# Down projections by seven products per 2x2 block, with low weight parts added in transit and one PSUM pool

## The chip, the core and the metric

One core of a Trainium2 chip runs the whole program in one launch. The engines are PE (the matrix engine, with its weight loads shown as PEld), DVE, ACT and POOL (element-wise work) and SP (which issues DMAs); ACT and POOL can issue DMAs too. The metric is the device time of one execution in microseconds, lower is better.

## What is computed

512 tokens with 1024 features pass two model blocks of two layers each. In the reference, cut to what matters here:

```python
def sqrelu_mlp(h, w1, w2):                 # first block, both layers; 1024 -> 4096 -> 1024
    return jnp.square(jax.nn.relu(h @ w1)) @ w2
def swiglu(h, w_gate, w_up, w_down):       # second block, both layers; 1024 -> 2816 -> 1024
    return (jax.nn.silu(h @ w_gate) * (h @ w_up)) @ w_down
# first block, layer l:  x += conformer_conv or fox_attention
#                        x += memory_cross_attention
#                        x += sqrelu_mlp(rmsnorm(x, norm_ff_g[l]), ff_w1[l], ff_w2[l])
# second block, layer i: x += short_conv_mixer or dilated_attention_mixer
#                        x += swiglu(rms_norm(x, ffn_norm[i]), gate, up, down)
```

All of it is in 32-bit floats.

## The kernel before

Activations lie transposed: features on 128 partitions, 512 tokens along a row, so that `x` is eight tiles `x[0..7]` of 128x512. Every matrix product keeps 32-bit precision by three matmuls in the reduced format FP32R: operands are split into a high part (a rounded copy) and a low part (the value less its high part), and `mm3` (L173) issues high x high, high x low and low x high into one PSUM bank.

`load_weights` (L146) has SP load 1 MB of weights (eight row tiles, 256 columns) into `raw`, a ring of three buffers. `split_weights` (L163) makes the parts of each 128 columns: ACT copies the high part `whi` (L169), DVE subtracts the low part `wlo` (L170). `gemm_steps` (L182) takes two output tiles at a time: for each it issues 8 x 3 matmuls of 128x128 weights by 128x512 activations, then calls `evac`.

In `ff_sqrelu` (L694) the 4096 hidden features are taken in four chunks of eight tiles. For each chunk a first product (w1) fills `hid`: DVE scales and clips out of PSUM (L706), ACT squares (L708), and `split_act` makes `ahi` (ACT) and `alo` (DVE, L224). A second product (w2) then multiplies the chunk by 1024x1024 weights, and `residual` (L591) adds each of the eight results to `x` on DVE (L593). In `swiglu` (L718) the chunks have 8, 8 and 6 tiles, and gate and up products stand for w1. The w2 product of one chunk is called a down projection stage below: 8 x 8 x 3 = 192 matmuls of 512 columns.

PSUM has eight banks of 128x512. `banks(g, s, t)` (L111) is called where an attention or a convolution begins; it closes the pool of PSUM tiles and opens another with the new division. The first tile of a new pool waits until those of the pool before have been read.

The order of matmuls is that of the program (L91 to L95). That of the other engines is set by the framework's scheduler, from the dependences and its own cost estimates; each engine works off its list in order, an instruction that waits holds up those behind it. In `fox` (L1107) POOL issues the loads of `fr` and `fb` and multiplies `fr` by a gain (L1119); before, in its list, stand eight gain multiplies on attention weights (L782, in `parts_of`). `fw` (L1123) is made of `fr` by ACT and DVE and is the operand of the first matmuls there. The end of the first block is `last1` (L1283), which adds the last result (L1284) and scales it.

Of the kernel before, what the change touches and what calls it, by code (L numbers as in the profile page):

```python
# [9 lines left out]
F32 = mybir.dt.float32  # L10
# [72 lines left out]
def model_kernel(tc, a, c_mats, c_onehot, c_lnn, out):  # L83
# [24 lines left out]

    psum = {}

    def banks(g, s, t):  # L111

        if psum:
            psum["stack"].close()
        psum["stack"] = ExitStack()
        psum["pool"] = pool("ps", stack=psum["stack"], space=bass.MemoryType.PSUM)
        psum["bufs"] = {"g": g, "s": s, "t": t}

    def bank(tag="g"):
        return psum["pool"].tile([P, 512], F32, name="ps_" + tag, tag=tag, bufs=psum["bufs"][tag])  # L120

# [41 lines left out]
    def split_weights(view, shape):  # L163
# [18 lines left out]
    def gemm_steps(specs, acts, evac, first=False, norm=None):  # L182

        nk = len(acts)
        for c in range(0, len(specs), 2):
            w = prepare(specs[c : c + 2], nk)
            nm = len(w)  # L190
# [400 lines left out]
    def residual(st):  # L591
# [102 lines left out]
    def ff_sqrelu(l, st, last=None):  # L694
        nrm = Norm(st)
        with ExitStack() as s:
            ap = pool("fact", 22, s)
            fp = pool("fftmp", stack=s)
            h = [gained_act(hp_all, x[k], gain("norm_ff_g", l)[:, k : k + 1]) for k in range(KT)]
            st2 = Stats()  # L700
            for hc in range(FF1 // D):
                hid = []

                def evac(m, acc, hid=hid):
                    t = fp.tile([P, T], F32, name="t", tag="t", bufs=4)
                    nc.vector.scalar_tensor_tensor(t, acc, 0.0, nrm.b, op0=OP.max, op1=OP.mult)  # L706
                    u = fp.tile([P, T], F32, name="u", tag="u", bufs=4)
                    nc.scalar.activation(u, t, AF.Square)  # L708
                    hid.append(split_act(ap, u))

                gemm(cols(a["ff_w1"][l], 0, hc * D), h, evac, first=hc == 0, norm=nrm, hooks=nrm.hooks() if hc == 0 else ())
                final = hc == FF1 // D - 1
                gemm(
                    cols(a["ff_w2"][l], hc * D, 0), hid, (last or residual(st2)) if final else residual(None), first=True
                )
        return st2

    def swiglu(l, st, last=None, finish=None):  # L718
        nrm = Norm(st)
        banks(4, 2, 2)  # L720
        with ExitStack() as s:
            ap = pool("gact", 22, s)
# [3 lines left out]
            wg, wu, wd = a["ffn_w_gate_2"][l], a["ffn_w_up_2"][l], a["ffn_w_down_2"][l]  # L726
            m0 = 0
            for n in (8, 8, 6):
                hid = []
                for j in range(n):  # L730
                    c = (m0 + j) * P
                    res = {}

                    def evac(m, acc, res=res, hid=hid):
                        if m == 0:
                            t = fp.tile([P, T], F32, name="t", tag="t", bufs=4)
                            nc.vector.tensor_tensor(t, acc, nrm.b, op=OP.mult)  # L737
                            g = fp.tile([P, T], F32, name="g", tag="g", bufs=4)
                            nc.scalar.activation(g, t, AF.Silu)  # L739
                            nc.gpsimd.tensor_tensor(g, g, nrm.b, op=OP.mult)  # L740
                            res[0] = g
# [12 lines left out]
                m0 += n
        return st2

    def heads_attention(specs, fold, h, nrm, bias_of, hp, wo, prologue, ahead=0):
# [19 lines left out]
        def parts_of(owner, view, nk, width, f, cuts, pl, tag):  # L777
# [92 lines left out]
        def v_steps(grp):  # L870
# [9 lines left out]
            def products():  # L880
                flush(("v", grp))
                for tt in range(2):
                    b = bank("g")
                    for t2 in range(2):
                        t = tt * 2 + t2
                        for k in range(KT):
# [491 lines left out]
    def finish(specs, acts):  # L1378
# [78 lines left out]
```

## Time and profile before

| | |
|---|---|
| median of 3 runs | 2654.21 us (2652.49 to 2655.27) |
| profiled execution | 2655.16 us, its span 2653.4 us |
| PE busy | 2600.3 us (98%), 12521 matmuls |
| DVE, ACT, POOL busy | 1489.7 (56%), 1097.9 (41%), 548.8 us (21%) |
| share of PE in the chain that ended last | 82% |

The span is the time from the first to the last recorded instruction. The trace gives each instruction a start and a duration; matmuls are pipelined, so that their records overlap, and the distance from one start to the next tells what one costs. "Idle before" a group is the time in which its engine stood still just ahead of it, with the event that ended it. A granted clock of 1.00 is 2.4 GHz, 0.50 is 1.2 GHz. A DMA's landing is counted from its issue to its completion.

### The profile page before, as it was taken

The numbers are of one execution on the slowest core, as the hardware profiler recorded it, in microseconds if no ns is written. First come the engines' busy times: TensorE is split into PE (matmuls) and PEld (weight loads), VectorE is DVE, ScalarE is ACT, GpSimd is POOL, SyncE is SP. The second block draws the span as 40 slices with busy tenths as digits, with TensorE's granted clock in tenths as the row PEclk, the third lists the DMA queues.
The fourth block names the chain that finished last, engine by engine and source line by source line (L and its number), as shares of the span: only waits on it lengthen the run. The fifth ranks groups of instructions, "written<-read, shape, count | busy, mean of one in ns | idle before, by whom it ended". The sixth has DMA issues, their size and how long they took to land.

```text
span 2653.4 us, 32283 instructions
## 1 busy us (share of the span) xinstructions
PE 2600.3 (98%) x12521; PEld 2178.7 (82%) x12521; DVE 1489.7 (56%) x2215; ACT 1097.9 (41%) x1843; POOL 548.8 (21%) x585
## 2 busy tenths in 40 slices
PE   8999999999999999999999999999999999999999
PEld 6889888888878787888888788888888888788888
DVE  6995564433557887554344665433335777643333
ACT  6755443322437675342223322322224666422223
POOL 5862110000226532110000511211112221211111
PEclk9999999999999999999999999999999999999999
DMA  7255133333322222233333393333324232233331
GB/s 211 78 194 181 56 96 96 98 103 101 95 74 72 80 96 72 72 111 96 95 97 96 87 166 109 90 100 101 96 83 119 85 88 88 77 96 98 96 87 56
DMA packets 319320, 264.82 MB, mean 100 GB/s; under 512 B 6980, under 2 KB 304512, under 8 KB 319168
## 3 DMA queue, kind: packets, MB, share of 16 engines
q1 hardware_dynamic: 316112, 258.15, 33.4%
q10 hardware_dynamic: 2480, 4.33, 0.5%
q8 instruction: 99, 1.62, 0.3%
q0 software_dynamic: 576, 0.28, 0.1%
q14 instruction: 53, 0.43, 0.1%
HBM read 251.16 MB, written 11.57 MB: 99 GB/s over the span
## 4 chain that ended last, share of the span: by engine, by line
PE 82%; DVE 6%; POOL 4%; issue 4%; ACT 2%; DMA 1%; SPq 0%; ACTq 0%; POOLq 0%; DVEq 0%
PE ps_g L92 76%; PE ps_s L92 3%; POOL pa L433 2%; PE ps_t L92 2%; PE ps_t L95 1%; DVE wlo L170 1%; DVE ps_s L425 1%; DVE alo L236 1%; DVE x L593 1%; POOL sall L994 1%; POOL raw L782 0%; DVE x L938 0%; DMA raw<-in_conv_pw_w 0%; DVE wlo L795 0%; DVE x L1286 0%
## 5 line engine op out<-in xcount | busy, mean ns | idle before, releaser
L92 PE MATMUL ps_g<-ahi,whi 128*128 128x512 f32 x3052 | 1195.2, 392 | 10.8 <-DVE x L593 5.8
L92 PE MATMUL ps_g<-alo,whi 128*128 128x512 f32 x3052 | 1188.0, 389 | 1.6 <-DVE alo L236 1.6
L92 PE MATMUL ps_g<-ahi,wlo 128*128 128x512 f32 x3052 | 1188.0, 389 | 0.0
L169 ACT CAST whi<-raw 128x1024 fp32r<-128x1024 f32 (+2 forms) x384 | 384.1, 1007 | 1163.1 <-PE ps_g L92 1103.3
L92 PEld LDWEIGHTS ps_g<-ahi,whi 128*128 128x128 f32 x3052 | 574.7, 188 | 129.6 <-issue 11.1
L92 PEld LDWEIGHTS ps_g<-ahi,wlo 128*128 128x128 f32 x3052 | 574.2, 188 | 120.3 <-DVE wlo L795 0.2
L92 PEld LDWEIGHTS ps_g<-alo,whi 128*128 128x128 f32 x3052 | 574.8, 188 | 117.5 <-DVE alo L236 2.4
L170 DVE TENSOR_TENSOR wlo<-raw,whi 128x1024 fp32r<-128x1024 f32 (+2 forms) x384 | 462.7, 1210 | 75.5 <-ACT whi L169 70.8
L593 DVE TENSOR_TENSOR x<-ps_g,x 128x512 f32<-128x512 f32 x144 | 99.1, 689 | 337.5 <-PE ps_g L92 337.5
L260 POOL TENSOR_TENSOR ssq<-ssq,sq 128x512 f32<-128x512 f32 x78 | 119.4, 1531 | 609.2 <-issue 311.9
L740 POOL TENSOR_TENSOR g<-g,rb 128x512 f32<-128x512 f32 x44 | 74.2, 1687 | 555.2 <-ACT g L739 555.2
L706 DVE SCALAR_TENSOR_TENSOR t<-ps_g,rb 128x512 f32<-128x512 f32 x64 | 44.0, 691 | 161.0 <-PE ps_g L92 160.3
L782 POOL TENSOR_TENSOR raw<-raw,gcols 128x512 f32<-128x512 f32 x48 | 53.8, 1145 | 302.1 <-DMA raw<-in_kvf_w 302.1
L433 POOL TENSOR_TENSOR pa<-pa,pr 128x512 f32<-128x512 f32 x80 | 111.8, 1400 | 18.7 <-ACT pa L429 8.2
L744 DVE TENSOR_TENSOR u<-ps_g,g 128x512 f32<-128x512 f32 x44 | 30.4, 691 | 145.3 <-PE ps_g L92 141.1
L425 DVE SCALAR_TENSOR_TENSOR ps_s<-u,gcols,ps_s 128x512 f32<-128x512 f32 x152 | 104.2, 744 | 0.2
L994 POOL TENSOR_SCALAR sall<-sall,rs 128x512 f32<-128x512 f32 (+3 forms) x128 | 75.9, 605 | 128.5 <-DVE rs L993 117.4
L795 DVE TENSOR_TENSOR wlo<-raw,whi 128x512 fp32r<-128x512 f32 x128 | 94.4, 765 | 13.2 <-ACT whi L792 13.2
L792 ACT CAST whi<-raw 128x512 fp32r<-128x512 f32 x128 | 74.1, 620 | 53.3 <-PE ps_g L92 47.1
L737 DVE TENSOR_TENSOR t<-ps_g,rb 128x512 f32<-128x512 f32 x44 | 30.4, 691 | 112.8 <-PE ps_g L92 112.8
L236 DVE SCALAR_TENSOR_TENSOR alo<-x,gcols,ahi 128x512 fp32r<-128x512 f32 x64 | 82.3, 1299 | 13.8 <-ACT ahi L235 13.8
L224 DVE TENSOR_TENSOR alo<-u,ahi 128x512 fp32r<-128x512 f32 x116 | 81.7, 707 | 2.7 <-ACT ahi L223 2.7
(244 smaller groups left out, 2838.0 us busy)
## 6 DMA issues: line engine op xcount, KB each, us to landing
raw<-in_ff_w SPq DMA_DIRECT2D x64, 1024.0 KB, 5.0
raw<-in_ffn_w_gate SPq DMA_DIRECT2D x44, 512.0 KB, 4.0
raw<-in_ffn_w_up SPq DMA_DIRECT2D x44, 512.0 KB, 5.3
raw<-in_ffn_w_down SPq DMA_DIRECT2D x16, 1024.0 KB, 5.0
raw<-in_conv_pw_w SPq DMA_DIRECT2D x16, 512.0 KB, 5.4
raw<-in_mem_wk SPq DMA_DIRECT2D x8, 1024.0 KB, 5.1
raw<-in_mem_wv SPq DMA_DIRECT2D x8, 1024.0 KB, 5.9
raw<-in_mem_wq SPq DMA_DIRECT2D x8, 1024.0 KB, 4.9
```

The lines of the kernel that those rows point to most:

```text
L92: tc.keep_in_program_order(nc.tensor.matmul(*args, **kw))
L169: nc.scalar.copy(hi, view)
L170: nc.vector.tensor_tensor(lo, view, hi.bitcast(F32), op=OP.subtract)
L224: nc.vector.tensor_tensor(lo, src, hi.bitcast(F32), op=OP.subtract)
L236: nc.vector.scalar_tensor_tensor(lo, src, g, hi.bitcast(F32), op0=OP.mult, op1=OP.subtract)
L260: nc.gpsimd.tensor_tensor(self.ssq, self.ssq, dst, op=OP.add)
L425: nc.vector.scalar_tensor_tensor(acc, u[:, j : j + T], tapw(j), acc, op0=OP.mult, op1=OP.add)
L433: nc.gpsimd.tensor_tensor(pa, pa, pr, op=OP.add)
L593: nc.vector.tensor_tensor(x[m], acc, x[m], op=OP.add)
L740: nc.gpsimd.tensor_tensor(g, g, nrm.b, op=OP.mult)
L795: nc.vector.tensor_tensor(w[1][:, k0 : k0 + n, :], v, w[0][:, k0 : k0 + n, :].bitcast(F32), op=OP.subtract)
L994: pinned(nc.gpsimd.tensor_scalar(s, s, rs[:, i : i + 1], 1.0, op0=OP.mult, op1=OP.mult))
```

## The change

The down projections of all but the last chunk of each MLP (three in each `ff_sqrelu`, two in each `swiglu`, ten stages in all) are computed by a scheme of seven products. A hidden pair (two tiles of hidden features, index k) and an output pair (two output tiles, index j, four of them) form a 2x2 block of weights a11, a12, a21, a22; the tokens are taken in two halves of 256. Each block needs seven products, of sums of weights by sums of activations, instead of eight: 4 x 7 x 4 x 3 matmuls of 256 columns per stage.

`Hidden` makes the activations' sums (DVE) and their parts; the seven entries of `bhi` and `blo` are the four quarters less one and four combinations. `Seven.weights` prepares one output pair. Two groups of weights enter as they are: b (a11) and a (a12 and a22). For these `split_by_transfer` has ACT write the high part, ACT write its negative into `wlo`, and POOL issue a DMA that adds the weights, read once more from DRAM, onto it. The other groups, c and d, are sums, made in place in `raw` (POOL one, DVE three) and split as before. Results go to `x` or to accumulators `acc`, and `combine` adds these to `x` during the first product of the last chunk.

All eight PSUM banks are now tiles of one pool that stays open; `banks` only deals them out anew, the least recently used first. In the fox stage the gain multiplies of one key/query pair and that of `fr` go from POOL to DVE.

The diff, cut to its core:

```diff
+    ps_pool = pool("ps", stack=psum, space=bass.MemoryType.PSUM)
+    by_use = list(range(8))
     def banks(g, s, t):
-        if psum:
-            psum["stack"].close()
...
+        free = list(by_use)
+        for tag, n in (("g", g), ("s", s), ("t", t)):
+            rings[tag], free = free[:n], free[n:]
     def bank(tag="g"):
...
+        return ps_pool.tile([P, 512], F32, name="ps_" + tag, tag=f"bank{i}", bufs=1)
+    def split_by_transfer(view, src, shape):
+        slot = "ab"[turn[0] // 2 % 2]
+        turn[0] += 1
+        hi = wsp.tile(shape, F32R, name="whi", tag="whi" + slot, bufs=2)
+        lo = wsp.tile(shape, F32R, name="wlo", tag="wlo" + slot, bufs=2)
+        nc.scalar.copy(hi, view)
+        nc.scalar.activation(lo, hi.bitcast(F32), AF.Identity, scale=-1.0)
+        nc.gpsimd.dma_start(lo, src, accum_op=OP.add)
+        return hi, lo
...
+    SEVEN = (
+        ("b", None, 0, "A", 1),
+        ("a", 0, 2, "B", 1),
+        ("a", 1, 6, "D", 1),
+        ("c", 1, 4, "C", 1),
+        ("c", 0, 3, "C", 0),
+        ("d", 1, 5, "A", 0),
+        ("d", 0, 1, "B", 0),
+    )
+    class Hidden:
...
+        def quarters(self):
+            f = self.raw
+            d = self.ap.tile([P, 4, HALF], F32, name="bdif", tag="bdif", bufs=1)
+            nc.scalar.copy(self.hi[:, 0:3, :], f[:, 1:4, :])
+            nc.vector.tensor_tensor(
+                d[:, 0:2, :], f[:, 1:3, :], f[:, 0:1, :].to_broadcast([P, 2, HALF]), op=OP.subtract
+            )
+            nc.vector.tensor_tensor(d[:, 2, :], f[:, 2, :], d[:, 0, :], op=OP.add)
+            nc.vector.tensor_tensor(d[:, 3, :], d[:, 2, :], f[:, 3, :], op=OP.subtract)
+            nc.scalar.copy(self.hi[:, 3:7, :], d)
+            for part, src in ((slice(0, 3), f[:, 1:4, :]), (slice(3, 7), d)):
+                nc.vector.tensor_tensor(
+                    self.lo[:, part, :], src, self.hi[:, part, :].bitcast(F32), op=OP.subtract
+                )
+    class Seven:
...
+        def weights(self, src, r0, j, h):
+            raw = load_weights([(src, r0, 2 * j * P), (src, r0, (2 * j + 1) * P)], 2 * h)
...
+            w = {
+                "b": split_by_transfer(a11, rows[:, :, 0, 0:P], [P, h, P]),
+                "a": split_by_transfer(odd, rows[:, :, 1, :], [P, h, 2 * P]),
+            }
+            nc.gpsimd.tensor_tensor(a21, a11, a21, op=OP.subtract)
+            nc.vector.tensor_tensor(a22, a22, a21, op=OP.subtract)
+            nc.vector.tensor_tensor(a11, a22, a11, op=OP.add)
+            nc.vector.tensor_tensor(a12, a12, a22, op=OP.subtract)
+            w["c"] = split_weights(even, [P, h, 2 * P])
+            w["d"] = split_weights(odd, [P, h, 2 * P])
+            return w
+        def add(self, src, r0, hid):
+            h = len(hid)
+            for j in range(KT // 2):
+                w = self.weights(src, r0, j, h)
...
+                order = [(i, k) for i in range(7) for k in range(h)]
+                if j == 0:
+                    order.sort(key=lambda ik: 2 if ik[0] > 4 else ik[1] == h - 1)
+                for i, k in order:
...
+                    act = (hid[k].hi[:, b, :], hid[k].lo[:, b, :])
...
+                    mm3(ps[name][:, half * HALF : (half + 1) * HALF], wk, act, opens, closes)
+                    if closes:
+                        self.evac(j, name, ps[name])
...
     def ff_sqrelu(l, st, last=None):
...
+                if final:
+                    gemm(cols(a["ff_w2"][l], hc * D, 0), parts, last or residual(st2), first=True)
+                else:
+                    seven.add(a["ff_w2"][l], hc * D, hid)
...
+                if owner[:2] == ("kq", 1):
+                    nc.vector.tensor_tensor(v, v, by, op=OP.mult)
+                    return
...
-            nc.gpsimd.tensor_tensor(fr, fr, gk.unsqueeze(2).to_broadcast([P, KT, 16]), op=OP.mult)
+            nc.vector.tensor_tensor(fr, fr, gk.unsqueeze(2).to_broadcast([P, KT, 16]), op=OP.mult)
```

Line numbers of the changed kernel are its own: L170 and L169 become L176 and L175, L706 becomes L852, L782 becomes L945 (L943 on DVE), L224 becomes L243.

POOL's list from the norm ahead of the first MLP on. Before, nothing of the MLP stands between the norm's sums (L260, L278) and the gain multiplies of the fox stage (L782):

```order
L260 TENSOR_TENSOR ssq_3295<-ssq_3295,sq_3467 128x512
L278 TENSOR_TENSOR rtm_3569<-ms_3567,mhalf_76 128x4
L782 TENSOR_TENSOR raw_5807<-raw_5807,gcols_86 128x4x128 x4
L260 TENSOR_TENSOR ssq_3510<-ssq_3510,sq_5550 128x512
L260 TENSOR_TENSOR ssq_3510<-ssq_3510,sq_5590 128x512
```

Now, in the same place, the subtraction in place on a raw weight (L686, four buffers' names for the four output pairs) and the adding DMAs (L187, a pair of b and a for each output pair) of the first seven-product stage:

```order
L686 TENSOR_TENSOR raw_3827<-raw_3827 128x4x128
L297 TENSOR_TENSOR rtm_3569<-ms_3567,mhalf_76 128x4
L686 TENSOR_TENSOR raw_3943<-raw_3943 128x4x128
L686 TENSOR_TENSOR raw_4059<-raw_4059 128x4x128
L187 DMA wlo_3830<-in_ff_w2 128x4x128
L187 DMA wlo_3835<-in_ff_w2 128x4x256
L686 TENSOR_TENSOR raw_4175<-raw_4175 128x4x128
L187 DMA wlo_3946<-in_ff_w2 128x4x128
L187 DMA wlo_3951<-in_ff_w2 128x4x256
L187 DMA wlo_4062<-in_ff_w2 128x4x128
L187 DMA wlo_4067<-in_ff_w2 128x4x256
```

Twelve such instructions come in for each of the ten stages. The subtraction for the fourth output pair (`raw_4175`) stands ahead of the transfers for the second (`wlo_3946`, `wlo_3951`).

DVE's list at the end of w1 in the first chunk. Before: the last two hidden tiles out of PSUM (`t`), their low parts (`alo`), and low parts of the next weights (`wlo`), then the first residual adds:

```order
L706 SCALAR_TENSOR_TENSOR t_3791<-ps_g_3765,rb_3603 128x512
L170 TENSOR_TENSOR wlo_3896<-raw_3893,whi_3895 128x1024
L224 TENSOR_TENSOR alo_3796<-u_3793,ahi_3795 128x512
L706 SCALAR_TENSOR_TENSOR t_3823<-ps_g_3766,rb_3603 128x512
L170 TENSOR_TENSOR wlo_3900<-raw_3893,whi_3899 128x1024
L224 TENSOR_TENSOR alo_3828<-u_3825,ahi_3827 128x512
L593 TENSOR_TENSOR x0_78<-ps_g_3841,x0_78 128x512
L593 TENSOR_TENSOR x1_79<-ps_g_3842,x1_79 128x512
```

Now: the last pair's tiles go to `braw_3789`, the sums to `bdif_3819`, the low parts to `blo_3788`; the low parts of groups c and d of the first output pair (`wlo_3844`, `wlo_3848`) lie among them:

```order
L852 SCALAR_TENSOR_TENSOR braw_3789<-ps_g_3762,rb_3602 128x512
L176 TENSOR_TENSOR wlo_3844<-raw_3827,whi_3843 128x1024
L665 TENSOR_TENSOR blo_3713<-bdif_3744,bhi_3712 128x1024
L852 SCALAR_TENSOR_TENSOR braw_3789<-ps_g_3792,rb_3602 128x512
L176 TENSOR_TENSOR wlo_3848<-raw_3827,whi_3847 128x1024
L658 TENSOR_TENSOR bdif_3819<-braw_3789 128x512
L665 TENSOR_TENSOR blo_3788<-braw_3789,bhi_3787 128x768
L661 TENSOR_TENSOR bdif_3819<-braw_3789,bdif_3819 128x256
L662 TENSOR_TENSOR bdif_3819<-bdif_3819,braw_3789 128x256
L665 TENSOR_TENSOR blo_3788<-bdif_3819,bhi_3787 128x1024
L720 TENSOR_TENSOR x1_79<-x1_79,ps_g_3871 128x256
L687 TENSOR_TENSOR raw_3943<-raw_3943 128x4x128
```

The low part of the last combinations (`blo_3788<-bdif_3819`) is now the last of six instructions behind the second tile.

POOL's list at the start of the fox stage, before, with the eight multiplies ahead of `fr`'s:

```order
L1116 DMA fr_5794<-in_kvf_w 128x8x16
L1118 DMA fb_5796<-in_fgate_b 128x16
L834 MEMSET kl_5962 64x512 x2
L782 TENSOR_TENSOR raw_5981<-raw_5981,gcols_86 128x4x128 x4
L782 TENSOR_TENSOR raw_6116<-raw_6116,gcols_86 128x512 x4
L260 TENSOR_TENSOR ssq_3510<-ssq_3510,sq_5754 128x512
L1119 TENSOR_TENSOR fr_5794<-fr_5794,gcols_86 128x128
L278 TENSOR_TENSOR rtm_5904<-ms_5902,mhalf_76 128x4
```

And now, where POOL keeps one set of four:

```order
L1280 DMA fr_6434<-in_kvf_w 128x8x16
L1282 DMA fb_6436<-in_fgate_b 128x16
L995 MEMSET kl_6598 64x512 x2
L945 TENSOR_TENSOR raw_6752<-raw_6752,gcols_86 128x512 x4
L279 TENSOR_TENSOR ssq_3506<-ssq_3506,sq_6394 128x512
```

The other four and `fr`'s own multiply stand in DVE's list now.

## Rows read from the trace of the kernel before

**Rows 1.** Page, span, busy time by engine and granted clock in 40 slices.

```profile
span 2653.4 us, 32283 instructions
...
PE 2600.3 (98%) x12521; PEld 2178.7 (82%) x12521; DVE 1489.7 (56%) x2215; ACT 1097.9 (41%) x1843; POOL 548.8 (21%) x585
...
PEclk9999999999999999999999999999999999999999
```

**Rows 2.** Windows, MLP stretches: us; PE, PEld, DVE, ACT, POOL busy (instructions); clock; DMA; GB/s.

```profile
408.00:738.00 330.00, 330.00 (x1457) 273.30 (x1457) 145.37 (x163) 106.87 (x139) 17.09 (x13) 1.00 0.31 97
...
2293.00:2640.00 347.00, 347.00 (x1562) 288.49 (x1560) 135.93 (x154) 100.07 (x125) 43.88 (x27) 1.00 0.30 85
```

**Rows 3.** Windows, one down projection of one hidden chunk.

```profile
438.70:482.20 43.50, 43.50 (x193) 36.04 (x192) 15.79 (x17) 9.49 (x10) 0.00 (x0) 1.00 0.32 97
```

**Rows 4.** Timeline, PE, 512-column matmuls: start, duration, engine, line, operation, operands.

```profile
450.03 0.39 PE L92 MATMUL ps_g<-ahi,whi 128*128 128x512 f32 x1
450.25 0.39 PE L92 MATMUL ps_g<-alo,whi 128*128 128x512 f32 x1
```

**Rows 5.** Waits of PE: instruction <- awaited line, us, times, longest.

```profile
PE ps_g L92 <- DVE x L593: 5.8, 7, 1.5
...
PE ps_g L92 <- DVE x L1284: 5.1, 1, 5.1
...
PE ps_s L92 <- DVE fw L1123: 3.8, 1, 3.8
```

**Rows 6.** Timeline, PE, 256-column matmuls.

```profile
213.76 0.28 PE L92 MATMUL ps_g<-whi,mhi 128*128 128x256 f32 x1
213.88 0.28 PE L92 MATMUL ps_g<-wlo,mhi 128*128 128x256 f32 x1
```

**Rows 7.** Page, costliest groups: weight loads, mean ns after the busy time.

```profile
L92 PEld LDWEIGHTS ps_g<-ahi,whi 128*128 128x128 f32 x3052 | 574.7, 188 | 129.6 <-issue 11.1
```

**Rows 8.** Timeline, POOL, start of the fox stage.

```profile
741.53 1.00 POOL L1116 DMA_DIRECT2D fr<-in_kvf_w  x1
742.53 0.57 POOL L1118 DMA_DIRECT2D fb<-in_fgate_b  x1
...
744.21 8.03 POOL L782 TENSOR_TENSOR raw<-raw,gcols 128x512 f32<-128x512 f32 x8
```

**Rows 9.** Groups by line and shape: busy us, mean ns, idle before.

```profile
L170 DVE TENSOR_TENSOR wlo<-raw,whi 128x1024 fp32r<-128x1024 f32 x336 | 425.8, 1273 | 75.5 <-ACT whi L169 70.8
L169 ACT CAST whi<-raw 128x1024 fp32r<-128x1024 f32 x336 | 351.0, 1052 | 1046.8 <-PE ps_g L92 999.2 <-issue 33.2 <-DMA raw<-in_conv_w_in 7.2
...
L706 DVE SCALAR_TENSOR_TENSOR t<-ps_g,rb 128x512 f32<-128x512 f32 x64 | 44.0, 691 | 161.0 <-PE ps_g L92 160.3 <-ACT rb L289 0.7
...
L708 ACT ACTIVATE u<-t 128x512 f32<-128x512 f32 x64 | 40.2, 629 | 1.7 <-DVE t L706 1.5
...
L170 DVE TENSOR_TENSOR wlo<-raw,whi 128x768 fp32r<-128x768 f32 x16 | 15.1, 954 | 0.0
...
L224 DVE TENSOR_TENSOR plo<-ps_t,phi 128x256 fp32r<-128x256 f32 x32 | 13.2, 412 | 0.0
```

**Rows 10.** DMA: queue totals; issues with KB each, median us to landing.

```profile
q1 hardware_dynamic: 316112, 258.15, 33.4%
...
raw<-in_ff_w SPq DMA_DIRECT2D x64, 1024.0 KB, 5.0
...
raw<-in_mem_wo SPq DMA_DIRECT2D x16, 512.0 KB, 3.5
...
tb<-gd SPq DMA_DIRECT2D x16, 256.0 KB, 2.7
```

**Rows 11.** Windows, after PE's pauses at fox start and block boundary.

```profile
755.60:761.20 5.60, 5.53 (x13) 2.98 (x14) 0.01 (x1) 0.00 (x0) 0.00 (x0) 0.50 0.72 187
1492.30:1495.20 2.90, 2.88 (x7) 2.32 (x8) 2.43 (x2) 0.98 (x2) 1.91 (x5) 0.50 0.41 105
```

**Rows 12.** Timeline, DVE, start of the fox stage.

```profile
745.13 9.68 DVE L795 TENSOR_TENSOR wlo<-raw,whi 128x512 fp32r<-128x512 f32 x2
```

More of the change, by code (lines that the diff above doesn't have):

```diff
@@ L190, in gemm_steps @@
             nm = len(w)
-            acc = [bank("g") for _ in range(nm)]
+            acc = {}
             outer = c == 0 and first
@@ L597, in residual, with flat, __init__, place @@
         return evac
+    SEVEN = (
[7 more added lines that the diff above has]
+    )
+    HALF = T // 2
+    def flat(v):
+        return v.rearrange("p a b -> p (a b)")
+    class Hidden:
+        def __init__(self, ap):
+            self.ap = ap
+            self.hi = ap.tile([P, 7, HALF], F32R, name="bhi", tag="bhi", bufs=4)
+            self.lo = ap.tile([P, 7, HALF], F32R, name="blo", tag="blo", bufs=4)
+            self.raw = ap.tile([P, 4, HALF], F32, name="braw", tag="braw", bufs=3)
+        def place(self, e):
+            return flat(self.raw[:, 2 * e : 2 * e + 2, :])
+        def tile(self, e):
+            hi, lo = (flat(z[:, 2 * e : 2 * e + 2, :]) for z in (self.hi, self.lo))
+            split_into(hi, lo, self.place(e))
+            return hi, lo
+        def quarters(self):
[12 more added lines that the diff above has]
+                )
@@ L696, in ff_sqrelu @@
         with ExitStack() as s:
-            ap = pool("fact", 22, s)
+            banks(6, 0, 2)
+            ap = pool("fact", stack=s)
             fp = pool("fftmp", stack=s)
@@ L700, in ff_sqrelu, with evac @@
             st2 = Stats()
+            seven = Seven(fp)
             for hc in range(FF1 // D):
-                hid = []
-                def evac(m, acc, hid=hid):
-                    t = fp.tile([P, T], F32, name="t", tag="t", bufs=4)
-                    nc.vector.scalar_tensor_tensor(t, acc, 0.0, nrm.b, op0=OP.max, op1=OP.mult)
[L707 to L715, printed above, removed]
+                hid, parts = [], []
+                final = hc == FF1 // D - 1
+                def evac(m, acc, hid=hid, parts=parts, final=final):
+                    if m % 2 == 0:
+                        hid.append(Hidden(ap))
+                    t = hid[-1].place(m % 2)
+                    nc.vector.scalar_tensor_tensor(t, acc, 0.0, nrm.b, op0=OP.max, op1=OP.mult)
+                    nc.scalar.activation(t, t, AF.Square)
+                    if final:
+                        parts.append(hid[-1].tile(m % 2))
+                    elif m % 2:
+                        hid[-1].quarters()
+                hooks = nrm.hooks() if hc == 0 else ()
+                if final:
+                    hooks = [(8 + 12 * j, lambda j=j: seven.combine(j)) for j in range(KT // 2)]
+                gemm(cols(a["ff_w1"][l], 0, hc * D), h, evac, first=hc == 0, norm=nrm, hooks=hooks)
+                if final:
+                    gemm(cols(a["ff_w2"][l], hc * D, 0), parts, last or residual(st2), first=True)
+                else:
+                    seven.add(a["ff_w2"][l], hc * D, hid)
         return st2
@@ L719, in swiglu @@
         nrm = Norm(st)
-        banks(4, 2, 2)
+        banks(6, 0, 2)
         with ExitStack() as s:
-            ap = pool("gact", 22, s)
+            ap = pool("gact", stack=s)
             fp = pool("gtmp", stack=s)
@@ L735, in evac @@
                         if m == 0:
[L736 to L739, printed above, removed]
+                            nc.vector.tensor_tensor(g, acc, nrm.b, op=OP.mult)
+                            nc.scalar.activation(g, g, AF.Silu)
                             nc.gpsimd.tensor_tensor(g, g, nrm.b, op=OP.mult)
[L741 removed]
@@ L751, in swiglu @@
-                gemm(cols(wd, m0 * P, 0, n_cols), hid, (last or residual(st2)) if final else residual(None), first=True)
-                if n_cols < KT:
-                    finish(cols(wd, m0 * P, n_cols * P, KT - n_cols), hid)
+                            nc.vector.tensor_tensor(g, acc, g, op=OP.mult)
+                            if final:
+                                parts.append(hd.tile(e))
+                            elif e:
+                                hd.quarters()
+                    first = m0 + j == 0
@@ new lines, in swiglu @@
+                    hooks = nrm.hooks() if first else ()
+                    if final and j < KT // 2:
+                        hooks = [(4, lambda j=j: seven.combine(j))]
+                    gemm([(wg, 0, c), (wu, 0, c)], h, evac, first=first, norm=nrm, hooks=hooks)
+                if final:
+                    n_cols = 6 if finish else KT
+                    gemm(cols(wd, m0 * P, 0, n_cols), parts, last or residual(st2), first=True)
+                    if finish:
+                        finish(cols(wd, m0 * P, n_cols * P, KT - n_cols), parts)
+                else:
+                    seven.add(wd, m0 * P, hid)
@@ L883, in products @@
                     b = bank("g")
+                    own = by_use[-1]
+                    held.add(own)
                     for t2 in range(2):
@@ L891, in products @@
                                 evac(tt, b)
+                                held.discard(own)
                             if k % 2 == 1:
```

75 lines of the change are left out of this document (55 added, 20 removed).

## Prediction

> **What bounds the kernel now.** I read the shares of the whole span first: PE, the matmul engine, is busy 2600.3 us of 2653.4 at the full clock [rows 1], so only matmul time and PE's own pauses can be bought. Next the four MLP stretches, cut out as windows: PE has no pause there (330.00 of 330, 347.00 of 347) and the clock is 1.00 [rows 2]. One down projection of one hidden chunk lasts 43.50 us, with DVE busy 15.79 and ACT 9.49 [rows 3]; its 512-column matmuls start 0.23 us apart [rows 4], and 43.50/192 = 0.2266 us. So the stretch that is changed is limited by the number and length of matmuls alone. Last the list of what PE waits for: 5.8 us in 7 waits on DVE's residual adds (L593), 5.1 us in one wait on L1284, 3.8 us in one wait on `fw` (L1123) [rows 5]. These three are touched by the other parts of the change.
>
> **Fewer products.** Ten stages (3 of 4 chunks in each `ff_sqrelu`, 2 of 3 in each `swiglu`) change from 192 matmuls of 512 columns to 4 x 7 x 4 x 3 = 336 of 256 columns. The trace has 256-column matmuls with new weights each, 0.12 us apart (213.76, 213.88 and so on through the stretch) [rows 6]. So a stage becomes 336 x 0.120 = 40.3 us, 3.2 less; ten stages: -32 us. One loaded weight now serves 0.12 us of streaming where a load record lasts 188 ns [rows 7]; by the spacing in rows 6 loads overlap enough, and I charge nothing for it.
>
> **What the new stage must prepare.** For each output pair j (a quarter stage, 10.1 us): POOL subtracts 128x512 in place (1.00 us: eight take 8.03 [rows 8]) and issues two adding transfers, about 0.8 us each (1.00 and 0.57 for the two issues in rows 8). ACT makes six copies and negations, 0.63 (512 columns, as L708) to 1.05-1.15 (1024, L169) each, some 5.5 us; DVE makes three sums of 512 (0.69 each, as L706) and two low parts of 1024 (1.27 each) [rows 9], 4.6 us, and evacuates for about 2.5. Each engine fits into 10.1 us, so the sums, the evacuations and the 24 `combine` operations per MLP are charged nothing: the rest of 10.1 us covers them. The cover is thinner than before: DVE goes from 16 of 43.5 us to about 29 of 40.3. What counts is then latency, at three places. E is the end of w1's last matmul.
>
> Place 1, start of a stage. PE has 15 x 3 x 0.12 = 5.4 us on hidden pairs 0 to 2, then 0.8 us on the first two products of pair 3, and then needs the low part of its 1024-column combination: at E+6.2. DVE's queue to it, by the order: L852 0.69, a weight's low part L176 1.27, L658 0.7, L665 on 768 columns 0.95, L661 and L662 0.42 each (the nearest row is 0.41), then ACT's high part 1.05 and DVE's low part 1.27: 6.8, and some 0.4 for six handoffs, 7.2 [rows 9]. PE waits 1.0 us. Behind that low part on DVE stand the next pair's sums, which are not due yet.
>
> Place 2, from j=0 to j=1 (two groups of weights enter unsummed: b, 256 KB, used by the first product, and a, 512 KB, by the second and third). On POOL the subtraction on the fourth raw weight stands ahead of j=1's adding transfers. Only three raw buffers exist; the fourth load starts when DVE has read j=0's raw (E+2.2), lands after 5.0 (the 1 MB load, rows 10) and is subtracted by E+8.4. Both transfers of j=1 queue behind it: b is issued by E+9.2, a by E+10.0. PE wants b at E+11.3 and a at E+12.7. A plain copy of such a size lands in 2.7 us (256 KB) and 3.5 us (512 KB) [rows 10]: b at 11.9, a at 13.5, 0.8 us late in sum.
>
> Place 3, twice per stage, from j to j+1. `a`'s buffers come free after 3/7 of a block and are wanted again at 8/7: 5/7 x 10.1 = 7.2 us, for ACT's copy 1.05, the negation 1.15 (estimated from L708, 0.63 for 512 columns), the issue 0.8 and handoffs 0.3. So a landing of up to 3.9 us is free, and every us above it is PE's.
>
> No adding transfer is in the trace, so its landing is the unknown. From below: as the plain transfers, 3.5 and 2.7 (0.8 us per stage and place 1, so 2628 in the sum below; quicker ones would leave place 1, 2620). From above: each byte handled twice or three times at the rate of the loads. Queue 1 moved 258.15 MB with 33.4% of the 16 engines' 2653.4 us [rows 10], so 291 GB/s: 512 KB are 1.8 us of its 3.5. Doubled: 5.3; tripled: 7.1. I take 4.0 for a and 2.9 for b, nearest to the plain rows of the same size. Then place 1 costs 1.0, place 2 1.3 (b 0.8 late, a 0.5 more), place 3 2 x 0.1: 2.5 per stage, +25 in ten stages.
>
> **Side parts.** One PSUM pool: before, closing a pool held the first matmul of the next stage until the last evacuation. At the block boundary PE stands 5.1 us for L1284 [rows 5], then runs 7 matmuls at granted clock 0.50, the 1.2 GHz level [rows 11]. After the change that stage starts on free banks, and only its own last activation could hold it: -5 (0 to -6). The seven L593 waits: -2 of 5.8. Fox start: POOL runs eight gain multiplies for 8.03 us ahead of `fr`'s [rows 8]; DVE's low parts stand through that (9.68 us for two) [rows 12], PE waits 3.8 us for `fw` [rows 5], and 13 matmuls follow at clock 0.50 in 5.6 us, 2.7 more than at 1.00 [rows 11]. After, four multiplies and `fr`'s go to DVE: POOL's `kl` and four multiplies end some 4 us earlier, and `fw` is ready at about 751, before PE wants it: -6.4 (0 to -6.5). DVE's part, five multiplies, lies in its free time behind residual adds that PE doesn't wait for. Together -13.
>
> **Sum.** The profiled execution took 2655.2 us (span 2653.4), 1 us above the median of the three runs, 2654.2. 2655.2 - 32 + 25 - 13 = 2635 us.
>
> **Rivals.**
> *The adding transfer pays twice.* It would have to read the old low part and the source, so a lands in 5.3 and b in 3.6. Place 2 then costs 2.6 (b 1.5, a 1.1 more), place 3 2 x 1.4, place 1 1.0: 6.4 per stage, +64. 2655 - 32 + 64 - 13 = 2674, taken as 2675: slower. A pause near those of rows 11 could also drop the clock, 2.7 us each time. It decides from a landing of about 4.8 us on. For it: the destination is data that must be fetched. Against it: at 291 GB/s no queue here is near its end, and the stage asks for 1.05 + 0.79 MB per 10.1 us, 182 GB/s.
> The Trainium skill, "Collectives: The Full Stack", section "The bandwidth ceiling: the fold count and why AG ≠ RS ≠ AR", says that an addition in the DMA path costs no cycles of its own but needs two source reads, and so runs at about half the rate of a copy. No run here shows it yet; by it, this rival's time is the forecast.
> *Gains eaten, no change.* Landing 4.5 and 3.2, or a DVE chain that runs longer than its parts at 70% load: 1.0 + 1.8 + 2 x 0.6 = 4.0 per stage, +40: 2655 - 32 + 40 - 13 = 2650. For it: three places each with under 1 us of slack.
> *The transfer is far dearer.* Three passes, or a fixed cost per run (512 runs of 512 B or 1 KB each): landing 7.1 and 4.5. Place 2 4.4, place 3 2 x 3.2, place 1 1.0: 11.8 per stage, +118: 2728, and more where the clock drops. Against it: the plain rows with the same runs show no such cost.
> *Short matmuls bound by weight loads.* At 188 ns each a stage would be 63 us, 20 more: about 2840. Rows 6 speak against it outright.
> *The side parts don't come*, because other waits take their place: forecast + 13, 2648, inside the range.
>
> **Chances.** Forecast 0.42 (own range 2618 to 2648); no change 0.20; twice 0.23; dearer 0.12; the others 0.03. A change under 0.2% (5.3 us) can't be told from none here. Faster takes the forecast, a third of the no-change case and a bit of the others, 0.50; same 0.13; slower 0.37. The range goes from 2612 (transfers as quick as plain, no pause but place 1) to 2692 (twice, with some clock lost); the dearest case and a little below are left out.
>
> **What would show it.** Spacing of 256-column matmuls in the new stages (0.120 or not); the landing of the 80 adding transfers (at most 4 us, or 5.3, or 7); PE's waits by name: `blo` once per stage near 1 us, the b and a low parts at j=1 and later; the granted clock of the MLP stretches staying 1.00; no wait on `fw` and none of 5 us at the block boundary. The forecast is wrong if PE's idle time in a new stage exceeds 3.2 us.

## The result, and where the time went

The changed kernel takes 2698.41 us (median of 4 runs, 2693.71 to 2705.09) against 2654.74 us: ratio 1.0171, 95% interval [1.0151, 1.0191]. It is 44 us slower, where 2635 was forecast, and lies 6 us above the range. The profiled execution took 2705.09 us, the longest of the four.

The page of the changed kernel, the lines that answer to [rows 1], and its two largest DMA queues:

```profile
span 2703.3 us, 35878 instructions
...
PE 2598.0 (96%) x13961; PEld 2241.4 (83%) x13961; DVE 1718.1 (64%) x2604; ACT 1272.0 (47%) x2035; POOL 698.9 (26%) x700
...
q1 hardware_dynamic: 316112, 258.15, 32.6%
q0 software_dynamic: 42816, 31.74, 8.5%
```

PE is busy for almost as long as before (2598.0 and 2600.3 us), with 1440 matmuls more, but the span grew by 50 us. What PE waits for, where before no weight stood in the list [rows 5]:

```profile
PE ps_g L92 <- DMA wlo<-in_ff_w: 38.5, 24, 3.2
PE ps_g L92 <- DMA wlo<-in_ffn_w_down: 20.2, 16, 2.5
...
PE ps_g L92 <- DVE blo L665: 4.8, 10, 0.6
...
PE ps_s L92 <- DVE fw L1287: 1.4, 1, 1.4
```

The adding transfers, `wlo`, hold PE for 58.7 us in 40 waits, four per stage as laid out. Place 1 (`blo`) costs 4.8 in ten stages. `fw` fell from 3.8 to 1.4, and the waits for L593 and L1284 are gone; the list also has 5.3 us for `alo`, where before had 1.6.

The issues, to be read against the plain transfers of [rows 10]:

```profile
raw<-in_ff_w SPq DMA_DIRECT2D x64, 1024.0 KB, 5.3
...
wlo<-in_ff_w POOLq DMA_DIRECT2D x24, 512.0 KB, 6.0
...
wlo<-in_ffn_w_down POOLq DMA_DIRECT2D x16, 512.0 KB, 6.0
...
wlo<-in_ff_w POOLq DMA_DIRECT2D x24, 256.0 KB, 4.9
...
wlo<-in_ffn_w_down POOLq DMA_DIRECT2D x16, 256.0 KB, 5.2
```

6.0 us for `a` and 4.9 to 5.2 for `b`; I had taken 4.0 and 2.9.

One stage, in windows (duration; PE, PEld, DVE, ACT, POOL busy; clock; DMA share; GB/s): the whole stage, the 3.4 us from the end of its first long pause on, and the last 4.6 us in which `a` of the second pair is under way:

```profile
531.80:581.40 49.60, 42.69 (x336) 41.58 (x335) 30.82 (x40) 22.84 (x25) 9.00 (x7) 0.97 0.65 144
545.20:548.60 3.40, 2.92 (x12) 2.63 (x12) 1.16 (x2) 0.59 (x1) 0.00 (x0) 0.50 1.06 178
545.60:550.20 4.60, 2.93 (x12) 2.63 (x12) 0.76 (x1) 1.25 (x2) 0.62 (x1) 0.67 1.09 247
```

The stage lasts 49.60 us, not 43.50 [rows 3] and not 40.3 plus 2.5. The clock falls to 0.50 in it. While the second pair's `a` is added, the DMA engines are full (share 1.09, as the view counts it; 0.32 over the stage in [rows 3]): in these 4.6 us the queue of the additions has 0.63 of it, that of a load of raw weights 0.46.

The same place on PE (start, duration, what it waited for): matmuls 0.12 us apart, then the pauses for b and a, and after the first a pace of 0.21 us:

```profile
542.67 0.28 PE L92 MATMUL ps_g<-bhi,whi 128*128 128x256 f32 x1
542.79 0.28 PE L92 MATMUL ps_g<-blo,whi 128*128 128x256 f32 x1
545.68 0.58 PE L92 MATMUL ps_g<-bhi,wlo 128*128 128x256 f32 x1 [2.61 <-DMA wlo<-in_ff_w]
546.06 0.41 PE L92 MATMUL ps_g<-bhi,whi 128*128 128x256 f32 x1
546.28 0.41 PE L92 MATMUL ps_g<-blo,whi 128*128 128x256 f32 x1
...
550.25 0.38 PE L92 MATMUL ps_g<-bhi,wlo 128*128 128x256 f32 x1 [1.64 <-DMA wlo<-in_ff_w]
```

And on POOL. The fourth raw weight's load was issued at 534.15 and landed 5.4 us later; the subtraction started at 539.76 (the profile names a DVE addition that ended in the same moment), and both transfers went out behind it, in 2.61 us:

```profile
539.76 1.29 POOL L686 TENSOR_TENSOR raw<-raw 128x512 f32<-128x512 f32 x1 [14.75 <-DVE x L720]
541.00 2.61 POOL L187 DMA_DIRECT2D wlo<-in_ff_w  x2
549.58 1.28 POOL L187 DMA_DIRECT2D wlo<-in_ff_w  x1 [5.97 <-ACT wlo L186]
```

Sum of the ten stages, from the first matmul's start to the last's: 492 us, where ten of before have 433. In them the matmuls at full clock need 402; the waits take 63.5 (58.7 + 4.8). Eight of the stages have 37.5 us at clock 0.50 between them; part of that is pause, and the matmuls that run in it lose 14 us against a pace of 0.12. The rest, 13 us, are longer steps before and behind the 50 pauses (as 550.25 to 550.47 above: 0.22 instead of 0.12). So the stages are 59 us longer; the profiled execution is 50 longer than that of before, which leaves 9 gained elsewhere.

### The profile page after: what moved, and what is told of

Same layout as the page of the kernel before. It is cut to its first block, busy times and chain, and to the rows that moved or that the text cites. A ratio compares the mean times of both kernels' runs of the same rounds, so it can differ in the third digit from the quotient of the medians.

```text
span 2703.3 us, 35878 instructions
## 1 busy us (share of the span) xinstructions
PE 2598.0 (96%) x13961; PEld 2241.4 (83%) x13961; DVE 1718.1 (64%) x2604; ACT 1272.0 (47%) x2035; POOL 698.9 (26%) x700
## 3 DMA queue, kind: packets, MB, share of 16 engines
q0 software_dynamic: 42816, 31.74, 8.5%
## 4 chain that ended last, share of the span: by engine, by line
PE 71%; DMA 8%; DVE 6%; issue 6%; POOL 5%; ACT 4%; SPq 0%; POOLq 0%; ACTq 0%; DVEq 0%
PE ps_g L92 65%; DMA wlo<-in_ff_w 4%; PE ps_s L92 3%; DMA wlo<-in_ffn_w_down 2%; POOL pa L452 2%; PE ps_t L92 2%; PE ps_t L95 1%; DVE wlo L176 1%; DMA raw<-in_ff_w 1%; DVE ps_s L444 1%; POOL sall L1158 1%; ACT whi L175 1%; ACT whi L185 1%; ACT wlo L186 1%; DVE alo L255 0%
## 5 line engine op out<-in xcount | busy, mean ns | idle before, releaser
L92 PE MATMUL ps_g<-ahi,whi 128*128 128x512 f32 x2176 | 857.8, 394 | 0.0
L92 PE MATMUL ps_g<-alo,whi 128*128 128x512 f32 x2176 | 851.7, 391 | 5.3 <-DVE alo L255 5.3
L92 PE MATMUL ps_g<-ahi,wlo 128*128 128x512 f32 x2176 | 851.4, 391 | 0.2 <-DVE wlo L956 0.2
L175 ACT CAST whi<-raw 128x1024 fp32r<-128x1024 f32 (+2 forms) x384 | 383.5, 1005 | 830.4 <-PE ps_g L92 697.0
L176 DVE TENSOR_TENSOR wlo<-raw,whi 128x1024 fp32r<-128x1024 f32 (+2 forms) x384 | 468.8, 1225 | 86.5 <-ACT whi L175 83.3
L92 PEld LDWEIGHTS ps_g<-ahi,whi 128*128 128x128 f32 x2176 | 410.7, 189 | 82.7 <-ACT whi L953 0.2
L92 PE MATMUL ps_g<-bhi,wlo 128*128 128x256 f32 (+1 forms) x1356 | 417.1, 308 | 58.8 <-DMA wlo<-in_ff_w 38.5
L92 PE MATMUL ps_g<-blo,whi 128*128 128x256 f32 (+1 forms) x1356 | 413.3, 305 | 4.8 <-DVE blo L665 4.8
L92 PE MATMUL ps_g<-bhi,whi 128*128 128x256 f32 (+1 forms) x1356 | 412.3, 304 | 0.0
L92 PEld LDWEIGHTS ps_g<-bhi,wlo 128*128 128x128 f32 x1356 | 265.4, 196 | 75.6 <-DMA wlo<-in_ff_w 43.7
L92 PEld LDWEIGHTS ps_g<-blo,whi 128*128 128x128 f32 x1356 | 265.5, 196 | 15.6 <-DVE blo L665 6.8
L92 PEld LDWEIGHTS ps_g<-bhi,whi 128*128 128x128 f32 x1356 | 265.8, 196 | 8.7
L686 POOL TENSOR_TENSOR raw<-raw 128x512 f32<-128x512 f32 x40 | 60.1, 1503 | 359.9 <-DMA raw<-in_ff_w 197.6
L852 DVE SCALAR_TENSOR_TENSOR braw<-ps_g,rb 128x512 f32<-128x512 f32 x64 | 44.1, 691 | 126.5 <-PE ps_g L92 125.9
```

Of the source, the lines that this page charges most:

```text
L92: tc.keep_in_program_order(nc.tensor.matmul(*args, **kw))
L175: nc.scalar.copy(hi, view)
L176: nc.vector.tensor_tensor(lo, view, hi.bitcast(F32), op=OP.subtract)
L686: nc.gpsimd.tensor_tensor(a21, a11, a21, op=OP.subtract)
```

## The experiments

Each is an edit of the changed kernel, except where another is named. A ratio is to the kernel before, timed beside it on the same chip.

### Transfers by themselves (e6_probes)

In the kernel before, each hidden pair of the MLPs also starts one transfer onto a scratch tile that nothing reads.

```diff
...
+        if kind == "copySP":
+            nc.sync.dma_start(dst, src)
+        elif kind[0] == "a":
+            nc.gpsimd.dma_start(dst, src, accum_op=OP.add)
+        else:
+            nc.gpsimd.dma_start(dst, src)
...
```

> The kernel before, with 76 transfers onto scratch tiles that nothing reads, one per hidden pair in the four MLPs, of seven kinds in turn: 512 KB adding (FP32R and 32-bit destination), 512 KB copying from POOL (both destinations), 512 KB copying from SP, 256 KB adding and copying from POOL (FP32R). Theory 'twice' (an adding transfer moves its bytes at half the rate): adding 512 KB lands in about 6.0 us, the copy from POOL in 4.0 to 4.3, from SP in 3.5 to 4; adding 256 KB 4.6 to 5, copy 3.1 to 3.4; the destination's type makes no difference. Rival 'POOL's queue' (transfers issued by POOL are slow whatever they do): the copies from POOL land in about 6.0 and 4.9 like the adding ones. Rival 'conversion' (writing FP32R is what costs): 512 KB into a 32-bit destination lands in about 4, into FP32R in 6, adding or not.

```profile
zaddR<-in_ff_w POOLq DMA_DIRECT2D x5, 512.0 KB, 6.4
zcopyR<-in_ff_w POOLq DMA_DIRECT2D x5, 512.0 KB, 5.4
zaddF<-in_ff_w POOLq DMA_DIRECT2D x5, 512.0 KB, 6.6
zcopyF<-in_ff_w POOLq DMA_DIRECT2D x5, 512.0 KB, 5.3
zcopySP<-in_ff_w SPq DMA_DIRECT2D x4, 512.0 KB, 5.8
...
zaddH<-in_ff_w POOLq DMA_DIRECT2D x4, 256.0 KB, 5.2
zcopyH<-in_ff_w POOLq DMA_DIRECT2D x4, 256.0 KB, 5.0
```

Adding 512 KB lands 1.0 to 1.3 us after a copy of it (1.5 us among the transfers from the other weights: 7.5 to 7.6 against 6.0 to 6.1), for FP32R (R) and 32-bit (F) destinations alike: the rival of conversion falls. For 256 KB (H) the difference is 0.2 us. All kinds land later than I expected, SP's copies too (5.8 against 3.5 in [rows 10]); what they met on their way was not resolved, but lateness isn't the addition's alone. Part of the difference lies at POOL: its issue of an addition takes 1.28 to 1.31 us, of a copy 0.76 to 0.81. With 4 to 7 of each kind from each weight this says that adding costs more, not how the cost grows.

### Sizes (e10_probe_sizes)

The same with adding and copying of 128 KB (rows of 256 B), 256 KB (rows of 512 B: half; 256 rows of 1 KB: tall) and 512 KB (1 KB).

```diff
...
+        kind, rows, width = (("short", 4, 64), ("half", 4, 128), ("tall", 2, 256), ("full", 4, 256))[probes[0] // 2 % 4]
+        adds = probes[0] % 2 == 0
...
```

> As run e6, with adding and copying transfers from POOL of four sizes onto a scratch tile: 512 runs of 256 B (128 KB), 512 runs of 512 B (256 KB), 256 runs of 1 KB (256 KB), 512 runs of 1 KB (512 KB). In run e6 the issue itself took 1.28 to 1.31 us for adding and 0.76 to 0.81 for copying, and 512 KB landed 1.0 to 1.6 us later. Theory 'issue and bytes' (0.5 us more at POOL, and the bytes at half rate, 0.9 us for 512 KB): adding is later by 1.4 us for 512 KB, by 1.0 for both 256 KB, by 0.7 for 128 KB. Rival 'per run': the same 1.4 us for the three of 512 runs, half as much for the 256 runs of 1 KB.

Medians over both weights, adding against copying: short 4.6 and 4.3, half 5.5 and 5.1, tall 6.1 and 5.0, full 7.0 and 5.8 us (9 or 10 of each; single ones spread over 1.4 to 3 us). The tall ones, with half the rows, lose 1.1 us and the half ones 0.4, which speaks against a fixed price per row. The price by bytes alone doesn't fit either (0.4 and 1.1 for the same bytes). With this spread neither is more than a hint. How the price is made up stays open.

### The 80 transfers as copies (e1_no_add)

```diff
-        nc.gpsimd.dma_start(lo, src, accum_op=OP.add)
+        nc.gpsimd.dma_start(lo, src)
```

> The changed kernel with the 80 transfers as plain copies (the low parts then hold whole weights); who waits for whom is unchanged. Theory 'twice': landing falls from 6.0 to about 4.2 (512 KB) and from 4.9 to about 3.3 (256 KB); PE's waits for them fall from 58.7 us to 15 to 20, all at the second output pair; some of the clock loss goes too; 2698 becomes 2640 to 2650. Rival 'POOL's queue': landing and waits stay, 2690 to 2700.

2644.47 us (2640.20 to 2646.65), ratio to before 0.9969 [0.9957, 0.998]. The page's second queue, the issues, and PE's waits:

```profile
q0 software_dynamic: 42816, 31.74, 5.8%
```

```profile
wlo<-in_ff_w POOLq DMA_DIRECT2D x24, 512.0 KB, 4.6
...
wlo<-in_ffn_w_down POOLq DMA_DIRECT2D x16, 512.0 KB, 4.3
...
wlo<-in_ff_w POOLq DMA_DIRECT2D x24, 256.0 KB, 3.6
```

```profile
PE ps_g L92 <- DMA wlo<-in_ff_w: 11.5, 11, 1.7
PE ps_g L92 <- DMA wlo<-in_ffn_w_down: 6.1, 7, 1.6
...
PE ps_g L92 <- DVE blo L665: 4.7, 10, 0.6
```

This is the main test. The same bytes on the same queue with the same dependences, without the addition: landing 4.3 to 4.6 and 3.6 us, waits 17.6 instead of 58.7, no stage with the clock at 0.50, and stages of 42.6 to 43.9 us. Some 54 us of the 2698 are the addition. The rival "POOL's queue" falls as the main cause; but these copies still land 0.8 to 1.1 us behind the plain rows that I had reckoned with, and a stage of 43.3 us on the mean is no gain over before. So the 8 us that e1 has over before lie outside the ten stages, as those of the side parts do (e5).

### POOL without the subtraction (e2_sub_on_dve)

```diff
-            nc.gpsimd.tensor_tensor(a21, a11, a21, op=OP.subtract)
+            nc.vector.tensor_tensor(a21, a11, a21, op=OP.subtract)
```

> The changed kernel with the subtraction L686 on DVE, so that POOL only issues the transfers. Theory 'POOL's order' (the second pair's transfers are late because they stand behind the subtraction on the fourth raw weight): the two waits at the second output pair, together 4.5 to 6 us per stage, fall by about 2 to 2.5; 2698 becomes 2670 to 2678. Rival 'rate alone': two transfers that are issued one behind the other share the rate, the wait falls by under 1 us per stage, 2688 to 2698.

2682.50 us, ratio 1.0113 [1.0096, 1.013]: 16 less than the changed kernel, between the two expectations. `wlo` waits are 45.7 us (58.7):

```profile
PE ps_g L92 <- DMA wlo<-in_ff_w: 26.9, 24, 2.9
PE ps_g L92 <- DMA wlo<-in_ffn_w_down: 18.8, 17, 1.9
```

In the second stage b was now issued before PE needed it and cost 0.6 us instead of 2.6, but a, behind it, 2.0 instead of 1.6. At the second pair the waits of all ten stages fall from 40.8 to 29.6 us, so POOL's order holds about a quarter of place 2, and the time at clock 0.50 falls from 37.5 to 17 us. The rest was not split further: the copies of e1, in POOL's old order, still wait 17.2 us there.

### Only b by transfer (e7_only_b)

```diff
+        if shape[2] == P:
+            nc.scalar.activation(lo, hi.bitcast(F32), AF.Identity, scale=-1.0)
+            nc.gpsimd.dma_start(lo, src, accum_op=OP.add)
+        else:
+            nc.vector.tensor_tensor(lo, view, hi.bitcast(F32), op=OP.subtract)
```

> The changed kernel with an adding transfer for b alone (256 KB); the low part of a is subtracted on DVE. Theory 'each group has its own slack' (a has 7.2 us less copy, negation and handoffs, b has 8.6): no waits between later output pairs; at the second pair only b is late, 2.3 to 2.8 us as in the changed kernel, and nothing of a behind it: stage about 43.5, 2645 to 2655 in all with the waits that run e4 shows in the last stage of an MLP. Rival 'the two transfers of a pair hold each other up': with a gone b lands in about 3.6 to 4 and its wait falls under 1.5 us: 2630 to 2640.

2658.47 us, ratio 1.002 [1.001, 1.0029]. Waits for `wlo` transfers are 20.1 us in 12, ten of them at the second pair (up to 3.0 us); b still lands in 4.8 to 4.9. It is a little over the expected 2655. Four stages have 17 us at clock 0.50 between them, whose matmuls lose 7 us. So b and a don't hold each other up by much, and the slack of place 3 is as worked out: b, with 8.6 us of it, is in time, a, with 7.2, was not.

### No transfer (e4_pool_b_dve_a, e3_dve_low)

In e4 POOL subtracts b's low part and DVE a's; in e3 DVE both.

```diff
-        nc.scalar.activation(lo, hi.bitcast(F32), AF.Identity, scale=-1.0)
-        nc.gpsimd.dma_start(lo, src, accum_op=OP.add)
+        (nc.gpsimd if shape[2] == P else nc.vector).tensor_tensor(lo, view, hi.bitcast(F32), op=OP.subtract)
```

> The changed kernel without any transfer: the low part of b is subtracted by POOL, that of a by DVE. Theory 'latency of the transfers is all that is lost': the waits for low parts go, place 1 stays at 0.7 us per stage, the clock stays up; 2655 - 32 - 13 + 7 = about 2617. Rival 'DVE has no room' (DVE's sums, low parts and evacuations fill the block): waits on wlo or blo of 2 to 3 us per stage come in their place, 2640 to 2655.

> The changed kernel without any transfer, the low parts of both b and a on DVE: 8.9 us of DVE work in a block of 10.1 us. Theory 'latency alone': as run e4, 2635 to 2642. Rival 'DVE has no room': waits on wlo in every stage, 2650 and more.

e4: 2638.26 us, ratio 0.9951 [0.9935, 0.9968]. e3: 2637.34 us, 0.9937 [0.9922, 0.9951], as expected for latency alone; e4 is 21 us over its forecast. e4's second and third stage of the first MLP, as windows:

```profile
522.01:563.33 41.32, 40.71 (x337) 40.30 (x335) 33.96 (x43) 17.71 (x19) 6.14 (x4) 1.00 0.37 116
607.00:653.58 46.58, 42.44 (x336) 41.83 (x335) 42.74 (x61) 17.34 (x19) 5.91 (x4) 0.96 0.27 84
```

All stages but an MLP's last take 40.8 to 41.3 us, place 1 included: the seven products give what was reckoned. The last stage lasts 45.3 to 46.6, with PE waiting for DVE's L176 (15.3 us in 8 waits over the four MLPs) and, in two of the four, 3.4 us at clock 0.50. In the third stage DVE is 92% busy (42.74 of 46.58 us), because the scheduler drew `combine` forward into it. DVE between a sum (L688) and the low part that PE waits for (L176), with three operations of `combine`:

```profile
620.03 0.68 DVE L688 TENSOR_TENSOR raw<-raw 128x512 f32<-128x512 f32 x1
620.64 1.52 DVE L732 TENSOR_TENSOR acc<-acc 128x256 f32<-128x256 f32 x1
622.08 0.68 DVE L733 TENSOR_TENSOR x<-x,acc 128x512 f32<-128x512 f32 x1
622.68 0.68 DVE L736 TENSOR_TENSOR x<-x,acc 128x512 f32<-128x512 f32 x1
623.28 1.21 DVE L176 TENSOR_TENSOR wlo<-raw,whi 128x1024 fp32r<-128x1024 f32 x1
```

The forecast of 2617 for e4 missed this; that `combine` costs nothing was wrong once nothing else delayed PE.

### combine on POOL (e8_combine_pool, e9_dve_low_combine_pool)

e4 and e3 with the six operations of `combine` on POOL.

```diff
-            nc.vector.tensor_tensor(acc[:, 0, :], acc[:, 0, :], acc[:, 1, :], op=OP.add)
+            nc.gpsimd.tensor_tensor(acc[:, 0, :], acc[:, 0, :], acc[:, 1, :], op=OP.add)
...
```

> Run e4 with the six operations of combine on POOL instead of DVE. In e4 the third stage of each MLP half lasts 46.6 us against 41.0 to 41.3 for the others, with waits of 2.1 and 1.8 us on wlo (L176) and combine's operations between the sums in DVE's list. Theory 'combine comes in the way': those stages fall to 41 to 41.5, four stages x 5 us: 2638 - 20 = about 2618. Rival 'it only moves the wait to POOL, where b's low part stands behind combine': 2630 to 2645.

> Run e8 with all low parts on DVE (POOL keeps the subtraction L686 and combine). In e4 and e8 DVE's L186 took 1.57 us where POOL worked beside it and 1.21 to 1.23 elsewhere. Theory 'the last stage's remaining waits come from DVE's list': DVE has 0.7 us more per block, the waits of 0.8 to 1.3 us in the last stage of an MLP grow to about 1.5, 2627 to 2632. Rival 'POOL beside DVE is what delays it': they vanish, about 2620.

e8: 2626.54 us (2622.80 to 2628.27), ratio 0.9893 [0.9879, 0.9908], faster than both kernels. e9: 2633.69, 0.9924 [0.9911, 0.9938]. PE's waits in e8, and the same two stages as of e4:

```profile
PE ps_g L92 <- DVE blo L664: 4.7, 10, 0.6
PE ps_g L92 <- DVE wlo L176: 3.3, 4, 1.2
```

```profile
521.87:563.19 41.32, 40.70 (x337) 40.29 (x336) 33.98 (x43) 17.70 (x19) 6.16 (x4) 1.00 0.36 116
606.85:649.46 42.61, 41.19 (x337) 40.41 (x335) 40.01 (x40) 17.45 (x19) 32.08 (x21) 1.00 0.29 93
```

The last stage falls from 46.58 to 42.61 us. In e9, where DVE has b's low part as well, 2.0 to 2.8 us of wait stay in each last stage (10.0 in 4), more than the 1.5 expected: DVE's list is the limit there, not POOL's company. e8 didn't reach 2618, since its four last stages still take 42.6 to 43.0 us, some 7 us more in sum than the others.

### The side parts alone (e5_side_parts)

The changed kernel with both MLPs as in the kernel before. What is left of the change, against the kernel before and cut:

```diff
+    ps_pool = pool("ps", stack=psum, space=bass.MemoryType.PSUM)
...
+        return ps_pool.tile([P, 512], F32, name="ps_" + tag, tag=f"bank{i}", bufs=1)
...
+                if owner[:2] == ("kq", 1):
+                    nc.vector.tensor_tensor(v, v, by, op=OP.mult)
...
+            nc.vector.tensor_tensor(fr, fr, gk.unsqueeze(2).to_broadcast([P, KT, 16]), op=OP.mult)
```

> The side parts alone: one PSUM pool, lazily taken accumulators, gain multiplies on DVE in the fox stage; both MLPs multiply as before, 192 matmuls of 512 columns. The sum of the prediction has -13 for this: 2655 - 13 = 2642, with no pause of 5 us at the block boundary and none of 3.8 on fw. From the traces of both kernels: the ten stages of the changed kernel last 492 us instead of 434, 58 more, and the whole 44 more, so that -14 is left for the side parts: 2640. Rival 'side parts bring nothing, the loss is all in other places': 2652 to 2656.

2643.78 us, ratio 0.9957 [0.9942, 0.9972]: -11, interval -7 to -15. -13 was in the sum. The wait for `fw` is 1.4 us as in the changed kernel, and the clock stays at 1.00 behind it. At the block boundary the 5 us are gone, with 0.4 us left, though the clock falls to 0.50 there as before, for 3.4 us (1491.0 to 1494.4). Where PE waited for L593 it now waits for `alo`: 5.3 us, against 7.4 for the two before.

## Why the prediction was wrong, step by step

**What bounds the kernel** and **fewer products** were right, with 256-column matmuls 0.12 us apart as in [rows 6]; a stage without late weights lasts 40.8 to 41.3 us (e4), 40.3 and place 1, against 43.5. The rival of weight loads falls with it.

**The landing of the adding transfers** is the step that failed. With it, and with POOL's order at place 2, the waits at the three places, +25 in the sum, came to 72 us, counted from one matmul's start to the next (6 at place 1, 44 at place 2, 21 at place 3). I took 4.0 and 2.9 us, "nearest to the plain rows of the same size", and it was 6.0 and 4.9 to 5.2. Two things lay in between. A copy by POOL's queue under these conditions takes 4.3 to 4.6 and 3.6 (e1), and the addition 1.3 to 1.7 us more on top. The plain rows were SP's; the trace had no POOL transfer above 80 KB, and that should have moved the value up, not left it at the lower end. The rival "pays twice" had the cause, the addition, and the sign, with 5.3 and 3.6 still too low; that it pays for a second read is not shown. By the page, 31.74 MB took 8.5% of 16 engines' 2703.3 us as additions, 138 GB/s, and 5.8% of 2641.2 as copies (e1), 207: two thirds of a copy's rate. The Trainium skill, "Collectives: The Full Stack", section "The bandwidth ceiling: the fold count and why AG ≠ RS ≠ AR", says half the rate because of two reads, of a reduce-scatter between cores in a ring. Here the direction is the same; about half (0.47) is what stands against SP's queue (293 GB/s), not against copies by the same queue.

**Place 3** behaved as worked out: 7.2 us less copy 1.05, negation 1.06 and handoffs. My sum took 0.8 us off for the issue as well, though landing is counted from the issue's start; so the free landing was 4.8, not 3.9, and 6.0 gives 1.2 us, twice a stage: 0.8 to 1.4 measured in 17 of 20, from one matmul's start to the next.

**Place 2** was mis-sized: 1.3 us forecast, 4.4 measured on the mean, by the matmuls' starts. Here too the issue was counted beside a landing that includes it; without that my own landings give 0.5. POOL's issues took 1.28 us each, not 0.8; its subtraction 1.3 to 1.5, not 1.0, and `a` took 8.4 us from its issue to its landing (541.8 to 550.2), while the additions, and towards its end a raw load, filled the DMA engines. e2 shows that POOL's order is a quarter of it.

**Place 1**: 1.0 us forecast, 0.5 to 0.7 measured.

**The clock** was in my text only as a remark on a rival, and in no sum. In the changed kernel eight of ten stages have 3.4 to 10.2 us at 0.50, 37.5 us in all, in which the matmuls lose 14 us; in e1, with pauses of up to 1.7 us, none has. Not every such pause does it: two stages of the changed kernel, with pauses of up to 2.4 and 2.2 us, stay at 1.00. But [rows 11] showed the price, and a mechanism that stops PE for 2 to 3 us had to be charged for it.

**Side parts**: -13 forecast, -11 measured. Right in sum; of the 6.4 us at the fox start some 5 came, since `fw` still costs 1.4.

**combine at no cost**: hidden behind later things in the changed kernel, whose last stages have no wait for L176, but 2.4 to 4.0 us in each last stage once they went (e4 against e8).

The corrected sum: 2655 - 32 (matmuls) + 63 (waits) + 14 (clock) + 13 (longer steps at the pauses) - 11 (side parts) = 2702; the profiled execution, from which these terms are read, took 2705, and the median is 2698.

## To carry to other kernels

Where a change hands a step to a kind of transfer that the trace doesn't hold, the forecast is set by that landing time: don't take it from the lower bound, and compare it with the slack between a buffer's release and its next use. PE's pauses of 2 us and more cost their length, and in eight of ten stages here a stretch at half clock as well. And when a late step is mended, look at what the scheduler had put beside it: here the best version has the seven products with low parts made by POOL and DVE and `combine` on POOL, 1.1% faster than before.

## What the runs showed of the hardware

An addition in transit took POOL 1.28 to 1.31 us to issue, a copy of the same shape 0.74 to 0.81, and it moved its bytes at 138 GB/s instead of 207. POOL's 128x512 operation took 1.00 us at the start of the fox stage (eight took 8.03, [rows 8]) and 1.50 on the mean on weights in the MLP (L686). DVE's low part of 1024 columns (L186) took 1.21 to 1.23 us alone and 1.57 to 2.29 beside a POOL operation (e8).
